# A hybrid trunk block on one core: squares ahead of the projection, and six up-projection units in front instead of four

## The chip, the cores and the metric

The kernel runs on one core of one Trainium2 chip. The core has a matrix engine (PE), a vector engine (DVE), an activation engine (ACT), a general engine (POOL), a queue engine that issues transfers (SP), and DMA engines between HBM and on-chip memory. Each engine works through its own list of instructions in order; semaphores make one wait for another. Matmul results land in eight accumulation banks. The metric is the device time of one execution in microseconds, the median of several runs. Lower is better.

## The reference

One layer of a hybrid block over x of 2048 rows by 1024 columns in float32, then a final RMSNorm:

```python
xn = rmsnorm(x, norm1_g[l])
z = xn @ w_in[l]
u_pool, zq, zf, zi, zo, zg = jnp.split(z, splits, axis=-1)
gates = jax.nn.sigmoid(zg + b_gate[l]).reshape(B, S, N_BRANCHES, D_MODEL)
ya = pool_mixer(u_pool, pool_w[l], pool_scale[l]) @ w_pa[l]
yb = hgrn2_mixer(zq, zf, zi, zo, lower_bounds[l], hgrn_norm_g[l]) @ w_pb[l]
merged = gates[:, :, 0] * ya + gates[:, :, 1] * yb
x = x + merged @ w_o[l]
x = x + conv_glu_ffn(rmsnorm(x, norm2_g[l]), w_up[l], conv_w[l], conv_b[l], w_down[l])
return rmsnorm(x, final_g)
```

The mixers are a causal pooling over windows of 2 to 16 rows and a gated linear recurrence. The feed-forward part (FFN) multiplies by w_up (1024 by 5632), applies a causal convolution of width 3, a SiLU gate, and multiplies by w_down (2816 by 1024).

## The kernel before

**Passes and stages.** The 2048 rows go through in two passes (b0 = 0 and 2) of 1024 rows, each two blocks of 512: the "first rows" and the "second rows". A pass runs proj_io (the columns of w_in for the recurrence's input and output gate), the other projections, the mixers, the output projection (wo), and then ffn: the up-projection in 22 units of 128 value and 128 gate columns, and the down-projection.

**Seven products.** Each product of two-by-two blocks (two halves of the contraction, two blocks of rows or columns) is done with seven block products, P1 to P7, instead of eight, in Strassen's manner. Each needs a form of the rows: P1 B11, P2 B21 (first rows alone), P6 T2, P5 T1, P7 T3, P4 T4, P3 B22 (all with second rows in them). forms_a_task makes B11 and B21, forms_b_task the other five. The weights, too, enter as quarters or sums of quarters.

**Precision.** Each operand is split into a rounded high part and the remainder (`split` for rows, `Stream.convert` for weights: a copy on ACT at line 205, a subtraction on DVE at line 206). A product is three matmuls, high by high, high by low, low by high. A step (one unit, one of P1 to P7) has four parts of three, twelve matmuls of 512 columns.

**Order by ticks.** Every sixth matmul calls tick(), which converts the next weight of the stream, at most LOOKAHEAD = 4 ahead of the step and with N_OPS = 6 buffers, and lets each waiting task emit its next piece. need() makes the task that builds the forms emit what a step needs before the step. What is emitted earlier has priority, and a scheduler then fixes the order of each engine's list. Working tiles are 82 "slots" of one pool (N_SLOTS).

**The opening.** At the end of the program text forms_of("x", 0, ...) makes the two tasks for the first 1024 rows: nxt[1] for the first rows and nxt[2] for the second. nxt[1] is stepped five times (squares, row norms, transposes of the first rows), the loads of the second rows are issued (load_rows(1)), and nxt[1] is run to its end. nxt[2] is not stepped there; the first tick inside proj_io does it. Its first step goes through norm_rows for all four tiles of 128 rows without a pause (lag 0): for each tile two squares with sums on ACT (row_rstd, line 635), a sum and the reciprocal root on POOL (lines 636, 628, 629), two scalings on DVE (line 649). It then waits for go_io, which proj_io sets at the second part of P2, and goes on with transposes on PE and the forms T2, T1, T3, T4 and B22. In proj_io the four results of P1 are copied out of their banks by ACT (io_e, line 1142) before P2 adds to the same banks.

**The FFN's start.** up_order gives the order of the steps. The N_HEADS = 2 first pairs of units, (0, 1) and (2, 3), lead: P1 and P2 of all of them come first, which want the first rows alone; then the other five products, pair by pair. The rest of the units follow interleaved, with a shift of seven steps. GO_AT = 5: from the sixth step on forms_b_task may go on with the second rows. P1's result is copied out (e1, line 1031), P2's too (h, through value, line 991); P6 and P7 leave u2 and u3 (lines 1033, 1037), P4 and P3 close (lines 995, 997). The convolution and the gate of a unit are put on a list, `work`, of which one item is taken per step.

**Names in the views.** x_ and m_ are the rows ahead of the projection and ahead of the FFN; x_f6h is the high part of the seventh tile of the first rows' forms, m_T23l the low part of T2's fourth; io_, fr_, gr_, ur_, up_, wo_ and dn_ are the products, with X, Z and V for the banks; ops are converted weights, raw loaded ones, kw and su weight sums kept in or made in DRAM.

Of the kernel before, what the change touches and what calls it, by code (L numbers as in the profile page):

```python
# [14 lines left out]
AF = mybir.ActivationFunctionType  # L15
# [43 lines left out]

N_SLOTS = 82  # L60
N_RUN = 3
N_HEADS = 2
GO_AT = 5
LEAD = 5
X_AT, X_AT2 = 1, 4
# [7 lines left out]
N_OPS = 6  # L73
# [5 lines left out]
def tile_trunk(  # L79
# [16 lines left out]
    pe, act, dve, pool, sp = nc.tensor, nc.scalar, nc.vector, nc.gpsimd, nc.sync  # L96
# [9 lines left out]
    def slot(name, cols=TB, dt=F32):  # L106
        return slots.tile([P, cols], dt, tag="s", name=name, padded_shape=[P, 528])
# [4 lines left out]
    def f32(ap):  # L112
        return ap.bitcast(F32)
# [26 lines left out]
    def join(task):  # L140
        while task.live:
            task.step()
# [14 lines left out]
    class Stream:  # L157
# [34 lines left out]
        def convert(self):  # L192
            j = len(self.tiles)
            key, fn, raws = self.ops[j]
            while any(r.tile is None for r in raws):
                self.load()
            store_kept()
            v = fn(f"w{j}")
            t = opsp.tile([P, 2, 512], F32R, tag="ops", name=f"ops{j}")
            n = int(np.prod(v.shape[1:]))  # L200
            hi, lo = t[:, 0, :n], t[:, 1, :n]
            if len(v.shape) == 3:
                hi = hi.rearrange("p (a b) -> p a b", a=v.shape[1])
                lo = lo.rearrange("p (a b) -> p a b", a=v.shape[1])
            self.mark = act.copy(hi, v)  # L205
            dve.tensor_tensor(lo, v, f32(hi), ALU.subtract)  # L206
            self.tiles.append((key, t))
            self.load_ahead()
# [21 lines left out]
    def behind(ins, other):  # L230

        tc.add_manual_dep(ins.ins, other.ins.name, mybir.DependencyInfo(
            mybir.DependencyClass.NoSync, mybir.DependencyReason.DATA), reason="behind")

    urgent = [None]

    def first(ins):

        urgent[0] = ins
# [68 lines left out]
    def store_kept():  # L308
        while keeping:
            sp.dma_start(*keeping.pop(0))  # L310
# [110 lines left out]
        return {p: (lambda p=p: plan(p)) for p in ORDER}  # L421

    def up_order():
        heads = [(0, 1), (2, 3), (4, 5)][:N_HEADS]
        res = [(m, p) for ms in heads for p in ("P1", "P2") for m in ms]
        res += [(m, p) for ms in heads for p in ("P6", "P5", "P7", "P4", "P3") for m in ms]

        rest = [(7 * m + 2 * i, m, p) for m in range(2 * N_HEADS, MF)
                for i, p in enumerate(ORDER)]
        return res + [(m, p) for _, m, p in sorted(rest)]  # L430

    def plan_ffn():
        units = {}
        for m, p in up_order():
            if m not in units:
                units[m] = sums_of_unit(w_up_t, m, MF + m,
                                        lambda p, m=m: sums["up"].of(m, SUM_OF[p]))
            fn, raws = units[m][p]()
            stream.op("up", fn, raws)
        plan_rows("dn", w_dn, R_DN, MF // 2)  # L440
# [67 lines left out]
    def load_rows(b):  # L508
        for j in range(NT):
            load_x_tile(b, j)  # L510
# [39 lines left out]
    junk = const.tile([P, 512], F32, tag="junk", name="junk")  # L550
# [6 lines left out]
    def setup_task():  # L557
        pool.memset(uhist, 0.0)
        pool.iota(inv[:, 3], pattern=[[1, 16]], base=1, channel_multiplier=0,
                  allow_small_or_imprecise_dtypes=True)  # L560
        for g, w in enumerate(WINDOWS):
            pool.tensor_scalar(inv[:, g], inv[:, 3], float(w), None, ALU.min)
        flat_inv = inv.rearrange("p a b -> p (a b)")
        dve.reciprocal(flat_inv, flat_inv)
        yield 1
        keys = [(h, h, 0, h) for h in (1, 2, 4, 16)]
        for t, off in ((0, 0), (1, 0)):
            pool.memset(fmask[:, t], 0.0)
            pool.affine_select(out=fmask[:, t], in_=fmask[:, t], compare_op=ALU.not_equal,
                               fill=1.0, base=off, pattern=[[-2, 64]], channel_multiplier=1)  # L570
        keys += [(8 * h + t, 2 * h, t * h, h) for h in (4, 16) for t in range(2)]
        for key, x, off, w in keys:
            nb = 64 // x
            mf = slot(f"mf{key}", 64)
            pool.memset(mf, 1.0)
            v = mf.rearrange("p (b h) -> p b h", h=x)
            pool.affine_select(out=v, in_=v, pattern=[[-2 * x, nb], [0, x]],
                               compare_op=ALU.is_ge, fill=0.0, base=-off, channel_multiplier=1)
            pool.affine_select(out=v, in_=v, pattern=[[2 * x, nb], [0, x]],
                               compare_op=ALU.is_ge, fill=0.0, base=off + w - 1,  # L580
                               channel_multiplier=-1)
            m8 = const.tile([P, 64], U8, tag=f"m{key}", name=f"m{key}")
            yield 2
            dve.tensor_copy(m8, mf)
            masks[key] = m8.rearrange("p (b h) -> p b h", h=x)
        for t in range(2):
            mf = slot(f"mfd{t}", 64)
            pool.memset(mf, 0.0)
            pool.affine_select(out=mf, in_=mf, compare_op=ALU.not_equal, fill=1.0, base=-t,
                               pattern=[[-2, 64]], channel_multiplier=1)  # L590
            m8 = const.tile([P, 64], U8, tag=f"md{t}", name=f"md{t}")
            yield 2
            dve.tensor_copy(m8, mf)
            masks[-1 - t] = m8.unsqueeze(1)
        pool.memset(hist, 0.0)
        for h in range(HEADS):
            pool.memset(state[h, 0], 0.0)
# [28 lines left out]
    def rstd_of(ssq, n, scale, name):  # L626
        r = small.tile([P, 4], F32, tag="rstd", name=name)
        pool.tensor_scalar(r[:, :n], ssq, scale, EPS, ALU.mult, ALU.add)  # L628
        pool.tensor_tensor(r[:, :n], r[:, :n], neghalf[:, :n], ALU.pow)
        return r  # L630

    def row_rstd(halves, junk, name):
        ss = small.tile([P, 4], F32, tag="ssq", name=name + "ss")
        for hf in range(2):
            act.activation(junk[hf], halves[hf], AF.Square, accum_out=ss[:, hf : hf + 1])
        pool.tensor_tensor(ss[:, 2:3], ss[:, 0:1], ss[:, 1:2], ALU.add)
        return rstd_of(ss[:, 2:3], 1, 1.0 / D, name + "r")

    def norm_rows(src, name, xs, after, lag=1):
        for j in range(NT):  # L640
            while (src, j) not in ready:
                yield 1
            halves = [xt[src, j, c] for c in range(2)]
            t = [slot(f"{name}xs{j}_{hf}") for hf in range(2)]
            r = row_rstd(halves, t, f"{name}{j}")
            if lag:
                yield lag
            for hf in range(2):
                dve.tensor_scalar(t[hf], halves[hf], r[:, 0:1], None, ALU.mult)
                xs[j, hf] = t[hf]  # L650
            after(j)
# [101 lines left out]
    def forms_of(kind, b, gain, after=lambda b: lambda j: None, early=False, go=lambda: True):  # L753
        forms = {k: [] for k in ("B11", "B21", "B22", "T1", "T2", "T3", "T4")}
        full = {k: [] for k in ("B11", "B21", "T2")}
        first = Task(forms_a_task((kind, b), gain, forms, full, after(b), early))
        late = Task(forms_b_task((kind, b + 1), gain, forms, full, after(b + 1), go))
        return forms, first, late
# [230 lines left out]
    def value(dst, a, ps):  # L989
        if a is None:  # L990
            act.copy(dst, ps)
            return
        t, how = a
        if how == "from":
            dve.tensor_tensor(dst, ps, t, ALU.subtract)  # L995
        else:
            dve.tensor_tensor(dst, t, ps, ALU.add if how == "add" else ALU.subtract)  # L997
# [382 lines left out]
    def ffn(b0, forms, late):  # L1380
# [15 lines left out]
        def emit_up(m):  # L1396
# [41 lines left out]
            def emit(s, hf, a, ps):  # L1438
                h = slot(f"h{b0}_{m}_{s}_{hf}", 2 + TB)
                hs[s, hf] = h  # L1440
                value(h[:, 2:], a, ps)
                first = (0, 0) if m >= 2 * N_HEADS else (1, 0)
                if (s, hf) == first:
# [103 lines left out]
    nxt = forms_of("x", 0, o_n1, early=True, go=lambda: go_io[0])  # L1547
    for _ in range(5):
        nxt[1].step()
    load_rows(1)  # L1550
    join(nxt[1])
    Task(setup_task())
    lg = cols[:, o_lb : o_lb + 4]
    dve.tensor_tensor(lbt[:, 0], lg, lg, ALU.subtract)
# [5 lines left out]
    for b in range(0, SEQ // TB, 2):  # L1560
# [4 lines left out]
        nxt = ffn(b, forms, late)  # L1565
# [50 lines left out]
```

## Time and profile before

| what | us |
|---|---|
| runs before (3) | 2573.06, 2574.07, 2575.15; median 2574.07 |
| the profiled execution | 2575.64 |
| its span, first to last instruction | 2573.9 |
| PE busy in it | 2519.3 |
| DVE, ACT, POOL busy in it | 1964.0, 1191.9, 851.5 |
| mean granted clock of PE | 0.993 of full |

A row of a timeline or group names start, duration, engine, line of the kernel, operation, and the tiles as out<-in, with shapes and a count; in brackets stands how long the engine was idle before it, and what ended that. PEld is the load of weights into PE. Matmuls overlap: one has a length of 0.39 us in the rows, while the next one starts 0.23 us behind it. Rows of waits and groups are sums over the whole span unless a stretch is given.

### The profile page before, as it was taken

How to read it: one execution, taken by the hardware profiler on the slowest of the kernel's cores; microseconds unless marked ns; L12 is line 12 of the kernel's file. 1: busy time of each engine (PE TensorE's matmuls, PEld its weight loads, DVE VectorE, ACT ScalarE, POOL GpSimd, SP SyncE). 2: the span in 40 equal slices, each digit the busy share in tenths (PEclk: the TensorE clock that was granted, in tenths of full speed). 3: DMA queues.
4: the chain of work that ended last, by engine and by line, in shares of the span. 5: the costliest groups of instructions: out<-in, count | busy, mean ns of one | idle time of the engine just before them, and what ended most of it. 6: DMA issues, size and time to landing. Idle time of an engine off the chain costs nothing.

```text
span 2573.9 us, 35491 instructions
## 1 busy us (share of the span) xinstructions
PE 2519.3 (98%) x11464; PEld 2057.0 (80%) x11464; DVE 1964.0 (76%) x3382; ACT 1191.9 (46%) x2244; POOL 851.5 (33%) x1209
## 2 busy tenths in 40 slices
PE   7899999999999999999999999999999999999998
PEld 6678888788788888878878888888887888888887
DVE  7878788478789777786486776775978987778844
ACT  5335434324555544554364354442355554445533
POOL 6534344031445333462141111200223433334502
PEclk9899999999999999999999999999999999999999
DMA  6787768767788888887364343356442454446942
GB/s 219 254 248 204 210 201 247 215 223 245 179 235 235 235 242 230 252 318 252 107 211 149 99 139 119 120 160 224 143 165 88 151 153 144 144 139 209 366 149 98
DMA packets 254058, 496.88 MB, mean 193 GB/s; under 512 B 26736, under 2 KB 43248, under 8 KB 253552
## 3 DMA queue, kind: packets, MB, share of 16 engines
q1 hardware_dynamic: 187968, 319.89, 38.5%
q0 software_dynamic: 41504, 110.64, 16.8%
q10 hardware_dynamic: 24400, 64.08, 7.3%
q8 instruction: 90, 1.47, 0.2%
q14 instruction: 96, 0.79, 0.1%
HBM read 384.94 MB, written 187.17 MB: 222 GB/s over the span
## 4 chain that ended last, share of the span: by engine, by line
PE 89%; DVE 5%; issue 2%; ACT 2%; DMA 1%; POOL 1%; SPq 0%; DVEq 0%; POOLq 0%; ACTq 0%
PE dn_P L145 16%; PE up_Z L145 14%; PE up_V L145 9%; PE up_X L145 9%; PE wo_P L145 6%; PE gr_Z L145 5%; PE pb L145 3%; PE pa L145 3%; PE gr_X L145 3%; PE gr_V L145 3%; PE fr_Z L145 3%; PE fr_V L145 2%; PE fr_X L145 2%; PE pl L867 1%; PE io_Z L145 1%
## 5 line engine op out<-in xcount | busy, mean ns | idle before, releaser
L205 ACT CAST ops<-raw 128x512 fp32r<-128x512 f32 x732 | 452.7, 620 | 792.9 <-PE dn_P L145 147.6
L206 DVE TENSOR_TENSOR ops<-raw,ops 128x512 fp32r<-128x512 f32 x732 | 555.4, 762 | 207.8 <-ACT ops L205 204.0
L1409 DVE SCALAR_TENSOR_TENSOR e<-h,cols,e 128x512 f32<-128x512 f32 x176 | 142.4, 812 | 30.8 <-ACT e L1407 26.5
L1407 ACT ACTIVATE e<-h,cols 128x512 f32<-128x512 f32 x176 | 142.4, 814 | 29.1 <-DVE h L997 21.0
L1412 DVE SCALAR_TENSOR_TENSOR e<-h,cols,e 128x512 f32<-128x512 f32 x176 | 133.7, 768 | 2.8
L805 POOL DMA_DIRECT2D g_P<-dg_P x154 | 83.3, 543 | 101.3 <-PE dn_P L145 28.5
L1103 POOL TENSOR_TENSOR gf_P<-e,e 128x512 f32<-128x512 f32 x44 | 65.6, 1493 | 153.3 <-DVE e L1418 98.8
L1103 POOL TENSOR_TENSOR gf_P<-gf_P,e 128x512 f32<-128x512 f32 x44 | 59.1, 1344 | 66.6 <-DVE e L1418 66.1
L1402 POOL COPY h<-h 128x2 f32<-128x2 f32 x88 | 39.5, 463 | 121.2 <-DVE h L995 119.2
L1404 POOL COPY hist<-h 128x2 f32<-128x2 f32 x88 | 38.8, 442 | 121.1 <-DVE h L997 119.4
L1416 ACT ACTIVATE e<-e 128x512 f32<-128x512 f32 x88 | 55.6, 632 | 46.2 <-DVE e L1412 46.0
L997 DVE TENSOR_TENSOR h<-up_u,up_V 128x512 f32<-128x512 f32 x88 | 60.0, 682 | 13.3 <-PE up_V L145 12.8
L1212 POOL TENSOR_TENSOR q<-q,qs 128x512 f32<-128x512 f32 x16 | 22.7, 1419 | 139.0 <-ACT qs L1211 127.9
L854 POOL COPY qm<-q 128x64 f32<-128x64 f32 x64 | 24.4, 404 | 117.7 <-DVE q L860 43.9
L1079 DVE TENSOR_TENSOR x<-x,wo_P 128x512 f32<-128x512 f32 x88 | 56.0, 675 | 8.3 <-PE wo_P L145 8.1
L1249 ACT ACTIVATE gt<-gt,cols 128x512 f32<-128x512 f32 x48 | 34.8, 725 | 57.5 <-DVE gt L997 35.1
L1079 DVE TENSOR_TENSOR ac<-ac,dn_P 128x512 f32<-128x512 f32 x72 | 47.3, 682 | 18.4 <-PE dn_P L145 16.5
L1103 POOL TENSOR_TENSOR yf_P<-ya,ya 128x512 f32<-128x512 f32 x16 | 21.1, 1322 | 117.3 <-DVE ya L1326 117.3
L628 POOL TENSOR_SCALAR ro<-so 128x4 f32<-128x4 f32 x16 | 3.2, 199 | 156.8 <-ACT junk L969 156.8
L1477 POOL TENSOR_TENSOR fss<-fss 128x1 f32<-128x1 f32 x16 | 6.6, 415 | 144.2 <-ACT fo L1467 144.2
L1432 POOL DMA_DIRECT2D dg_P<-gf_P x88 | 50.1, 569 | 8.5 <-POOL gf_P L1103 7.7
L1031 ACT COPY up_e<-up_X 128x512 f32<-128x512 f32 x44 | 25.8, 586 | 57.6 <-PE up_X L145 47.5
(1267 smaller groups left out, 8303.4 us busy)
## 6 DMA issues: line engine op xcount, KB each, us to landing
g_P<-dg_P POOLq DMA_DIRECT2D x154, 256.0 KB, 6.4
raw<-in_w_up_t SPq DMA_DIRECT2D x132, 256.0 KB, 3.1
raw<-in_w_in_t SPq DMA_DIRECT2D x98, 256.0 KB, 3.2
dg_P<-gf_P POOLq DMA_DIRECT2D x88, 256.0 KB, 3.8
raw<-in_w_io SPq DMA_DIRECT2D x68, 256.0 KB, 4.8
dg_P<-e SPq DMA_DIRECT2D x66, 256.0 KB, 3.2
raw<-in_w_dn SPq DMA_DIRECT2D x66, 256.0 KB, 4.5
x<-in_x SPq DMA_DIRECT2D x64, 256.0 KB, 5.1
```

The costliest lines, as they stand in the source:

```text
L145: count[1] = pe.matmul(*args, **kw)
L205: self.mark = act.copy(hi, v)
L206: dve.tensor_tensor(lo, v, f32(hi), ALU.subtract)
L805: eng.dma_start(t, d)
L997: dve.tensor_tensor(dst, t, ps, ALU.add if how == "add" else ALU.subtract)
L1079: dve.tensor_tensor(t, t, ps[j], ALU.add if sg > 0 else ALU.subtract)
L1103: pin(pool.tensor_tensor(t, x0, x1, op))
L1407: in_turn(act.activation(t, h[:, 2:], AF.Identity, bias=col(o_cb + mt), scale=col(o_cw + 4 * MF + mt)))
L1409: in_turn(second(dve.scalar_tensor_tensor(t, h[:, 1 : 1 + TB], col(o_cw + 2 * MF + mt), t, ALU.mult, ALU.add)))
L1412: dve.scalar_tensor_tensor(t, h[:, 0:TB], col(o_cw + mt), t, ALU.mult, ALU.add)
L1416: in_turn(act.activation(g, g, AF.Silu))
L1432: pool.dma_start(d, t)
```

## The change

N_HEADS goes from 2 to 3, so that units 0 to 5 lead: twelve steps of P1 and P2 instead of eight come before the first P6, and three pairs run through the other five products instead of two. The first step of nxt[2], with the squares and scalings of the second rows, is emitted in the opening, ahead of everything of the projection. And the first weight conversion from the seventh on (j >= N_OPS) is ordered behind the last of these squares (`opening`): `behind` puts the copy on ACT at line 205 later in ACT's own list, without a semaphore. This happens once in the program. No arithmetic is added or taken away.

```diff
-N_HEADS = 2
+N_HEADS = 3
...
             self.mark = act.copy(hi, v)
+            if j >= N_OPS and opening[0] is not None:
+                behind(self.mark, opening[0])
+                opening[0] = None
             dve.tensor_tensor(lo, v, f32(hi), ALU.subtract)
...
     urgent = [None]
+    opening = [None]
...
-        heads = [(0, 1), (2, 3), (4, 5)][:N_HEADS]
+        heads = [(0, 1), (2, 3), (4, 5), (6, 7)][:N_HEADS]
...
-            act.activation(junk[hf], halves[hf], AF.Square, accum_out=ss[:, hf : hf + 1])
+            ins = act.activation(junk[hf], halves[hf], AF.Square, accum_out=ss[:, hf : hf + 1])
+            if name == "x1_3":
+                opening[0] = ins
...
     load_rows(1)
     join(nxt[1])
+    nxt[2].step()
     Task(setup_task())
```

## The prediction

> **What bounds the kernel now.** I read the page first, then PE's waits, then stretches of time (windows), then the timelines of single engines.
>
> ```profile
> span 2573.9 us, 35491 instructions
> ...
> PE 2519.3 (98%) x11464; PEld 2057.0 (80%) x11464; DVE 1964.0 (76%) x3382; ACT 1191.9 (46%) x2244; POOL 851.5 (33%) x1209
> ...
> PE 89%; DVE 5%; issue 2%; ACT 2%; DMA 1%; POOL 1%; SPq 0%; DVEq 0%; POOLq 0%; ACTq 0%
> ```
>
> PE is busy for 98% and is 89% of the chain that ended last. The change takes no matmul away, so it can win only PE's idle time, 2573.9 - 2519.3 = 54.6 us, and stretches at half clock. The windows (the stretch, its length, PE's busy time with matmuls, granted clock, DMA share, GB/s) show where some of both lies:
>
> ```profile
> 653.52:664.62 11.10, 11.10 (x50) 1.00 1.05 245
> 676.44:694.15 17.71, 13.76 (x50) 0.90 0.85 174
> 694.15:707.77 13.62, 12.14 (x49) 1.00 0.46 153
> 1938.90:1955.29 16.39, 13.62 (x50) 0.90 0.21 65
> 1955.29:1968.95 13.66, 12.17 (x50) 1.00 0.24 78
> 16.85:29.74 12.89, 12.89 (x48) 0.87 0.69 250
> 29.74:52.31 22.57, 16.84 (x81) 0.92 0.39 124
> ```
>
> The edges are starts of steps. The first row is the free pace: four steps of twelve matmuls in 11.10 us, 0.231 each. The next two are the eight steps P6, P5 and P7, P4 of the first pair of FFN units; the two after them the same in the second pass. P6 and P5 lose 17.71 - 11.10 = 6.61 and 16.39 - 11.10 = 5.29; P7 and P4 lose 2.52 and 2.56. The last two rows are the opening: P1 of the first projection without a gap, then P2, which takes 22.57.
>
> **Six units lead.** PE's timeline names the first of these losses:
>
> ```profile
> 679.97 0.51 PE L145 MATMUL up_Z<-m_T23h,ops 128*128 128x512 f32 x1 [1.29 <-ACT m_T23h L606]
> 681.61 0.51 PE L145 MATMUL up_Z<-m_T23l,ops 128*128 128x512 f32 x1 [1.14 <-DVE m_T23l L607]
> 683.69 0.63 PE L145 MATMUL up_Z<-m_T21l,ops 128*128 128x512 f32 x1
> 688.29 0.50 PE L145 MATMUL up_V<-m_T11l,ops 128*128 128x512 f32 x1 [0.68 <-DVE m_T11l L607]
> 690.09 0.50 PE L145 MATMUL up_V<-m_T12l,ops 128*128 128x512 f32 x1 [0.84 <-DVE m_T12l L607]
> ```
>
> P6 wants form T2 of the second rows, whose four parts ACT, DVE and POOL make one behind the other:
>
> ```profile
> 666.39 0.69 ACT L723 ACTIVATE m_b<-m_t,negs 128x512 f32<-128x512 f32 x1 [0.46 <-PE m_t L655]
> 679.95 1.61 DVE L607 TENSOR_TENSOR m_T23l<-m_t,m_T23h 128x512 fp32r<-128x512 f32 x1
> 680.82 0.59 ACT L991 COPY h<-up_X 128x512 f32<-128x512 f32 x1
> 682.43 0.62 ACT L205 CAST ops<-raw 128x512 fp32r<-128x512 f32 x1 [1.02 <-issue]
> ```
>
> The chain ends at 679.95 + 1.61 = 681.56; PE reaches P6 at 676.44. The change puts four more steps, P1 and P2 of units 4 and 5, in front of that P6 and leaves GO_AT at 5, so the chain starts where it did and P6 comes 48 x 0.231 = 11.1 later, at 687.5: slack 6.0. T1 is wanted by P5 at 693.1 instead of 682 plus the stalls. T10 and T11 are emitted before that; T13 is still made at the last moment, at P5's first step, but is wanted there only at the tenth matmul, 2.1 later, against 0.6 + 0.7 of work. So I take the whole 6.61 and 5.29 away, 11.9.
>
> What it adds: no instruction, only an order. Units 4 and 5 hold four more tiles, e1 and h, and their P2 adds to the bank that e1's copy must first read. That copy comes behind the h copy that ends at 680.82 + 0.59 = 681.4, lasts as long, and P2 of unit 4 starts at 682.0: between 0, and 0.6 if the cast of the row after it goes first. I take 0.3 per pass. P7 and P4 keep their 2.5, since T3 and T4 are emitted at the same distance before use; bounds 0 (hidden too) and twice that. The sum streams (DRAM adds on ACT's and POOL's queues) are asked for later or at the same step: unit 4's first sum at step 32 instead of 29, unit 5's at 33 instead of 34. **Term: -11.9 + 0.6 = -11.3 us**, bounds -16.4 and -6.
>
> The slow clock is in it. Right behind the T23 stalls the matmuls are 0.63 long at a pace of 0.43, and the windows give 0.90; 0.10 of 17.71 and of 16.39 is 3.4 us in all. The Trainium skill, TensorE: Matmul & The Clock Gate, section "Why this matters for your kernels", asks for no PE-idle gaps over about 3 us, and these gaps are 1.3 and 1.1, so by its rule they would not cost the clock. The trace has the slow stretch behind this stall in both passes, so I go by the trace; the other reading is a rival below.
>
> **The squares and the tied conversion.** ACT, then POOL, in the opening:
>
> ```profile
> 24.93 0.62 ACT L205 CAST ops<-raw 128x512 fp32r<-128x512 f32 x1 [6.69 <-PE io_X L145]
> 25.45 0.68 ACT L663 ACTIVATE x_b<-x_t,cols 128x512 f32<-128x512 f32 x1
> 26.55 0.69 ACT L663 ACTIVATE x_b<-x_t,cols 128x512 f32<-128x512 f32 x1
> 31.42 0.62 ACT L635 ACTIVATE x_xs<-x 128x512 f32<-128x512 f32 x1
> 32.03 2.01 ACT L1142 COPY io_e<-io_X 128x512 f32<-128x512 f32 x4
> 26.22 0.62 POOL L604 TENSOR_SCALAR x_f6h<-x_b 128x512 fp32r<-128x512 f32 x1 [4.77 <-ACT x_b L663]
> 27.32 1.14 POOL L604 TENSOR_SCALAR x_f7h<-x_b 128x512 fp32r<-128x512 f32 x1 [0.48 <-ACT x_b L663]
> 40.20 0.54 POOL L629 TENSOR_TENSOR x_3r<-x_3r,neghalf 128x1 f32<-128x1 f32 x1
> 19.38 1.05 POOL L604 TENSOR_SCALAR x_f4h<-x_b 128x512 fp32r<-128x512 f32 x1
> ```
>
> The cast at 24.93 is the seventh (six are in flight, N_OPS). It holds ACT for 6.69 us until PE frees a pair, and two x_b copies, the eight squares and the four io_e copies queue behind it. Tied behind the last square, it lets them past: x_b at 18.2 and 18.8, squares from 19.4 to 19.4 + 8 x 0.61 = 24.4. Their rows have come by then:
>
> ```profile
> L504 SPq DMA_DIRECT2D x<-in_x x16: 327/328/432, 0.8 to 15.6; - x16
> DMA to landing us min/median/max: 3.4/5.3/6.0
> ```
>
> The last is issued at 15.6 and lands by 21.6, while the squares are in their fourth. The cast then still starts at 24.93, so its wait costs nothing; behind it on ACT are the eighth cast and io_e, on DVE its remainder, on SP the load that reuses its raw buffer, all on time. If the squares were late, the cover is long: P2 wants this pair at about 31, and cast and remainder take 1.4. The step moved ahead issues squares, sums, rstd and scalings; no DMA, and it passes none on SP or POOL.
>
> What PE gets:
>
> ```profile
> 32.74 0.71 PE L145 MATMUL io_X<-ops,x_f4h 128*128 128x512 f32 x2 [3.00 <-ACT io_e L1142]
> 42.96 1.41 PE L655 MATMUL x_t<-ident,x_xs 128*128 128x128 f32 x9 [0.94 <-DVE x_xs L649]
> 52.31 0.72 PE L145 MATMUL io_Z<-ops,x_T20h 128*128 128x512 f32 x2 [1.78 <-DVE x_t L712]
> 48.62 1.91 PE L655 MATMUL x_t<-ident,x_xs 128*128 128x128 f32 x16
> 90.08 1.19 PE L145 MATMUL io_Z<-ops,x_T40h 128*128 128x512 f32 x2 [4.31 <-DVE io_u L1148]
> ```
>
> io_e no longer waits for the squares, so P2 starts at 29.74, 3.0 earlier, and the half clock behind that gap (0.08 of 22.57, 1.8 us) goes. But P6 at 52.31 hangs on the second rows: rstd on POOL, scaling on DVE, transposes, T2. POOL works without a break from x_f7h (ends 28.46) through masks and weight sums to the last rstd at 40.74, so that row of work moves by what POOL waited for: 4.77 + 0.48 = 5.25, less 0.4 because x_f6h then runs beside DVE, as x_f4h does (1.05 instead of 0.62). **Term: -4.8 us.** The lower end is 0, if what follows eats it (rival 1). The upper end is 7.7, PE alone: P2 from 29.74 with 48 x 0.231 and two times 1.91 of transposes ends at 44.6, and 52.31 - 44.6 = 7.7. What is late next is DVE's u3, for which PE waits at 90.08. DVE is busy nearly all of the time from 44.5 to there, so I let its end move along with its start:
>
> ```profile
> 44.53:90.00 45.47, 44.06 (x58) 0.98 0.66 226
> ```
>
> **Sum**: -11.3 - 4.8 = -16.1. The profiled execution took 2575.64 (span 2573.9 and 1.7 around it) and would take 2559.5. The median of the runs is 1.6 lower, 2574.07, which gives **2558.0 us**.
>
> **Rivals.**
>
> 1. The opening gives its gain back: the 4.31 at 90.08 grows to 9.1, because weight sums and loads, not the second rows, set DVE's pace. For it: DVE is the engine waited for there. Against: those sums stand in the same queue and move too. Only the lead remains: 2574.07 - 11.3 = 2562.8.
> 2. The stall in the FFN moves on: T1 and T3 are emitted just before use and P7 is reached without the pause in which DVE caught up. Then only the T23 stalls with their clock go (2.4 + 1.7 per pass, 8.2 together) and P7 pays some 1.5 each, as much as T11 and T12 did: 2574.07 - 4.8 - 8.2 + 3 = 2564. Against: the 6.0 of slack.
> 3. The clock rule of above holds, and the slow stretches come anyway: 3.4 less, 2561.4.
> 4. Slower: the 82 slots run out. They are given out in program order, so one that isn't free holds all later ones. The seven forms take 56, six leading units 12 instead of 8, the pair at work about 10: 78 by my count, 74 before. From 83 on each evacuation of P4 and P3 waits for a convolution to free a slot, which is one ACTIVATE and two DVE operations of
>
> ```profile
> L1409 DVE SCALAR_TENSOR_TENSOR e<-h,cols,e 128x512 f32<-128x512 f32 x176 | 142.4, 812 | 30.8 <-ACT e L1407 26.5
> L1407 ACT ACTIVATE e<-h,cols 128x512 f32<-128x512 f32 x176 | 142.4, 814 | 29.1 <-DVE h L997 21.0
> ```
>
> some 2.4 us; eight per pass and two passes are 38: 2574.07 - 16.1 + 38 = 2596. For it: the work left over peaks at 12 items instead of 10. Against: four slots spare.
> 5. The order comes out otherwise and nothing is won: about 2574.
> 6. More: P7 and P4 lose their 2.5 as well, and the opening gives 7.7: 2574.07 - 11.9 - 5.1 - 7.7 = 2549.4.
>
> **How the numbers follow.** Forecast 0.57, rival 1 0.13, 2 0.09, 3 0.03, 4 0.07, 5 0.06, 6 0.05. The range runs from 2551, between forecast and rival 6, to 2566, past rivals 1 to 3; left out are rivals 4 to 6, 0.18. About 0.2%, 5 us, is what a measurement of this kernel can tell from no change. Faster by more: 0.57 + 0.13 + 0.09 + 0.03 + 0.05 = 0.87; within: 0.06; slower: 0.07.
>
> **What would show it.** Right: PE's waits without m_T23h and m_T23l; twelve up_X steps without a gap before the first up_Z; no half clock behind them; on ACT the eight squares ahead of the seventh cast and no 6.69 before it; P2 close to 29.7, P6 near 47.5. Wrong: PE idle at P7's start (rival 2), over 8 us before P4 of the projection (rival 1), evacuations on DVE that wait for e tiles (rival 4).

## The result and the profile after

| | before | after |
|---|---|---|
| runs | 2573.06, 2574.07, 2574.30, 2575.15 | 2558.99, 2559.36, 2560.58, 2565.47 |
| median | 2574.19 | 2559.97 |
| profiled execution, its span | 2575.64, 2573.9 | 2560.58, 2558.7 |
| PE busy | 2519.3 | 2514.9 |

The ratio is 0.9949, with a 95% interval of 0.9932 to 0.9967: 14.2 us less (8.5 to 17.5). Forecast were 16.1 less and 2558.0. Five more runs of the changed kernel beside the experiments gave a median of 2561.66 against 2572.57, ratio 0.9959 (0.9946 to 0.9971), 10.9 less (7.5 to 13.9). The forecast lies inside the first interval and outside the second. An estimate from the two is a gain near 13, which makes the forecast some three microseconds too good.

The FFN's start came out as the working has it. In the windows of the changed kernel (stretch, length, PE busy, ..., granted clock) the eight steps of the first pair now are:

```profile
681.63:692.76 11.13, 11.13 (x49) 8.93 (x48) 8.03 (x11) 6.09 (x11) 2.72 (x2) 1.00 0.94 271
692.76:706.42 13.66, 12.19 (x49) 8.70 (x48) 13.29 (x21) 7.46 (x13) 4.14 (x8) 1.00 0.46 154
1939.32:1950.40 11.08, 11.08 (x49) 8.94 (x48) 8.03 (x11) 6.10 (x11) 2.73 (x2) 1.00 0.32 108
1950.40:1964.03 13.63, 12.15 (x49) 8.70 (x48) 13.29 (x21) 7.37 (x13) 3.89 (x7) 1.00 0.24 79
```

P6 and P5 run at the free pace in both passes (11.13 and 11.08 instead of 17.71 and 16.39), at full clock. P7 and P4 kept their loss (13.66 and 13.63; before 13.62 and 13.66). PE's waits in the first pass, 640 to 730 us, show one new wait, for up_e (e1); the other three stood there before:

```profile
PE up_Z L145 <- DVE up_u L1043: 1.0, 2, 0.6
PE up_X L145 <- ACT up_e L1037: 0.3, 1, 0.3
PE up_Z L145 <- DVE m_T43l L611: 0.2, 1, 0.2
PE up_Z L145 <- DVE m_T42l L611: 0.2, 1, 0.2
```

No row names m_T23h, m_T23l, m_T11l or m_T12l any more. (The lines of the changed kernel stand 3 to 6 further down than before.) In the opening ACT does what was forecast:

```profile
18.97 0.68 ACT L639 ACTIVATE x_xs<-x 128x512 f32<-128x512 f32 x1
...
23.78 0.23 ACT L639 ACTIVATION_READ_ACCUMULATOR x_xs<-x 128x1 f32 x1
26.03 1.31 ACT L205 CAST ops<-raw 128x512 fp32r<-128x512 f32 x2 [2.02 <-PE io_X L145]
28.79 2.67 ACT L1148 COPY io_e<-io_X 128x512 f32<-128x512 f32 x4 [1.45 <-PE io_X L145]
```

The eight squares run from 18.97 to 24.0 (forecast 19.4 to 24.4), the cast waits behind them, and io_e waits for PE, no longer for the squares. P2 starts at 30.67 instead of 32.74, and not at 29.7 as forecast: P1 lay under two slow windows of the clock (16.0 to 22.8) where the kernel before had one (16.8 to 20.2). And of the second rows' gain less arrives at PE than on POOL. POOL's last rstd, then PE's timeline with the starts of P2 and P6 and the wait for u3:

```profile
35.74 0.59 POOL L633 TENSOR_TENSOR x_3r<-x_3r,neghalf 128x1 f32<-128x1 f32 x1
```

```profile
30.67 0.63 PE L145 MATMUL io_X<-ops,x_f4h 128*128 128x512 f32 x2
...
49.78 0.95 PE L145 MATMUL io_Z<-ops,x_T20h 128*128 128x512 f32 x2 [1.46 <-DVE x_t L718]
...
87.72 0.77 PE L145 MATMUL io_Z<-ops,x_T40h 128*128 128x512 f32 x1 [2.20 <-DVE io_u L1154]
```

The last rstd ends at 36.33 instead of 40.74, 4.4 earlier; P6 starts at 49.78 instead of 52.31, only 2.5 earlier.

**A gain that nobody forecast.** Both programs issue the same number of PE instructions, so the start of the n-th one can be compared. Up to 456 us the changed kernel is 3.1 ahead; at 470 it is 7.3 ahead. There the kernel before waited, in PE's and ACT's timelines:

```profile
463.56 0.50 PE L145 MATMUL gr_Z<-x_T30h,ops 128*128 128x512 f32 x1 [2.37 <-DVE gr_u L1033]
461.56 0.62 ACT L606 CAST mxs_2h<-mx 128x512 fp32r<-128x512 f32 x1 [7.95 <-DMA mx<-md]
```

A load of mx kept a cast on ACT waiting; its remainder stands ahead of gr_u on DVE, and PE waits for gr_u. The change touches none of these instructions.

### The profile page after: what moved, and what is told of

It is laid out like the page before. It is cut to its first block, busy times and chain, and to the rows that moved or that the text cites. A ratio compares the mean times of both kernels' runs of the same rounds, so it can differ in the third digit from the quotient of the medians.

```text
span 2558.7 us, 35497 instructions
## 1 busy us (share of the span) xinstructions
PE 2514.9 (98%) x11464; PEld 2053.2 (80%) x11464; DVE 1976.1 (77%) x3382; ACT 1189.7 (46%) x2244; POOL 861.4 (34%) x1209
## 3 DMA queue, kind: packets, MB, share of 16 engines
q0 software_dynamic: 41504, 110.64, 16.9%
## 4 chain that ended last, share of the span: by engine, by line
PE 90%; DVE 4%; DMA 2%; POOL 2%; issue 1%; ACT 1%; SPq 0%; DVEq 0%; POOLq 0%; ACTq 0%
PE dn_P L145 15%; PE up_Z L145 14%; PE up_V L145 10%; PE up_X L145 9%; PE wo_P L145 6%; PE gr_Z L145 5%; PE pb L145 3%; PE pa L145 3%; PE gr_X L145 3%; PE gr_V L145 3%; PE fr_Z L145 2%; PE io_Z L145 2%; PE pl L873 2%; PE fr_X L145 1%; PE fr_V L145 1%
## 5 line engine op out<-in xcount | busy, mean ns | idle before, releaser
L209 DVE TENSOR_TENSOR ops<-raw,ops 128x512 fp32r<-128x512 f32 x732 | 547.6, 751 | 192.4 <-ACT ops L205 187.5
L1415 DVE SCALAR_TENSOR_TENSOR e<-h,cols,e 128x512 f32<-128x512 f32 x176 | 150.7, 859 | 22.7 <-ACT e L1413 20.4
L1418 DVE SCALAR_TENSOR_TENSOR e<-h,cols,e 128x512 f32<-128x512 f32 x176 | 139.2, 798 | 2.7
```

The lines of the kernel that those rows point to most:

```text
L1415: in_turn(second(dve.scalar_tensor_tensor(t, h[:, 1 : 1 + TB], col(o_cw + 2 * MF + mt), t, ALU.mult, ALU.add)))
L1418: dve.scalar_tensor_tensor(t, h[:, 0:TB], col(o_cw + mt), t, ALU.mult, ALU.add)
```

## The experiments

All edits are against the changed kernel, except e8. The table adds up each profile against the first profile of before: how much earlier the same PE instruction starts, in us. "To 135" is the 450th instruction (134.7 us in that profile). The next columns are what is won from 456 to 470 (instructions 2060 to 2110), and across the two starts of the FFN (first up_X of the pass to instruction 3400, 651 to 765 us; first up_X of the second pass to instruction 9124, 1913 to 2025). The last column is the whole of it at PE's last matmul (2566), with the other stretches in it.

| kernel | to 135 | 456 to 470 | FFN 1 | FFN 2 | at the end |
|---|---|---|---|---|---|
| after | 3.3 | 4.2 | 5.9 | 4.8 | 15.3 |
| after again (e9) | 1.5 | 3.0 | 5.9 | 4.8 | 11.3 |
| before again (e8) | -2.5 | 4.2 | 0.0 | 0.0 | 2.4 |
| e1 lead alone | 0.0 | 2.8 | 5.9 | 4.6 | 13.8 |
| e2 squares alone | 3.5 | 2.3 | -0.3 | 0.9 | 3.4 |
| e3 no tie | -2.4 | -0.5 | 5.8 | 4.7 | 5.0 |
| e4 eight lead | 2.1 | -0.5 | 3.2 | 2.5 | 7.1 |
| e5 later chain | 5.9 | 2.6 | 2.4 | 0.3 | 9.3 |
| e6 T1 sooner | 1.9 | 0.3 | 7.7 | 6.8 | 13.2 |
| e11 T1 sooner, again | 1.5 | 4.2 | 7.8 | 6.8 | 16.9 |
| e7 masks later | 7.2 | -1.6 | 5.9 | 4.8 | 14.7 |
| e10 both | 4.6 | 4.2 | 7.9 | 6.8 | 21.8 |
| e12 sums on POOL | 3.5 | 2.9 | 6.0 | 4.7 | 11.7 |

Among kernels with the same FFN edit the two FFN columns repeat to 0.3. They jump only where the slow clock comes or stays away (e2's second pass, e5's first). The first two columns vary by 4 to 5 among kernels that run the same order of instructions up to there, since their edits all lie further on (after, e4, e5, e6, e9, e11). The last column is less than the four before it together: 2.9 less in the changed kernel, 3.0 in e2, 3.8 in e9, while e1 and e8 lose nothing. This goes in small pieces over the span, and its cause stays open.

### e1: the lead alone

```diff
-                opening[0] = ins
+                pass
...
-    nxt[2].step()
```

> The changed kernel without the early step and without the tie: six units lead, the opening is that of the kernel before. Theory: the two parts are independent, and the lead alone takes what the traces show at the two starts of the FFN, 6.0 and 4.8, so 2574.2 - 10.8 = 2563.4, with the first up_Z free of waits for m_T23h and m_T23l, a wait for up_e of 0.3 per pass, and the opening at the times of before (P6 near 52.3, u3 wait 4.3). Rival: the opening is worth nothing in the end, and the lead alone gives the whole 14 (2560). Second rival: the 2.37 of idle time and the half clock at 461 to 467, which the profile of before has and that of the changed kernel hasn't, belong to the kernel with the old opening: then this profile shows them again, otherwise they were one execution's transfers.

Measured: 2562.70 (2561.89 to 2567.48) against 2573.75, ratio 0.9957 (0.9944 to 0.9969), 11.05 less. The FFN columns are those of the changed kernel, the opening is that of before (P6 at 52.68, u3's wait 4.90). The time alone does not exclude the first rival, since the changed kernel's second measurement gained 10.9, no more than this. The trace speaks against it: the opening column is 0.0 here, and 1.5 or more wherever the squares are tied. The second rival falls: the stall at 461 is short here with the old opening (table: 2.8 of the 4.2 won).

### e2: the squares alone

```diff
-N_HEADS = 3
+N_HEADS = 2
```

> The changed kernel with four leading units: only the early step and the tie are left. Theory: the opening is worth the 3.2 that the traces show up to 146 us, so 2574.2 - 3.2 = 2571.0, and the stalls for m_T23h and m_T23l stand as before. Rival: the opening also takes away the stall at 461 (4.2), which then is missing here and gives 2566.8. Second rival: worth nothing, 2574.2.

Measured: 2571.36 (2570.52 to 2574.60, 11 runs) against 2573.75, ratio 0.9992 (0.9983 to 1.0000), 2.4 less, half of the forecast 4.8; the interval just touches no change. With e1's 11.05 that makes 13.4, which lies between the two measurements of the whole (10.9 and 14.2), so nothing here speaks against adding the parts.

### e3: the early step without the tie

```diff
-                opening[0] = ins
+                pass
```

> The changed kernel with the early step but without the tie: the seventh and eighth casts stand ahead of the last two x_b copies on ACT again. Theory: the tie is what frees ACT, the early step alone brings nothing, since the squares then still queue behind the 6.7 of waiting: a 6 to 7 us wait before the seventh cast, io_e's first copy at 31 or later, P6 near 52, time as with the lead alone, 2563.4. Rival: the early step alone does it, 2560.

Measured: 2565.98 (2563.66 to 2570.79), ratio 0.9962 (0.9949 to 0.9976): 3.3 above e1, so the early step alone brings nothing; whether it costs is not shown, since the two ranges of times overlap. ACT's timeline of e3:

```profile
26.25 0.62 ACT L205 CAST ops<-raw 128x512 fp32r<-128x512 f32 x1 [8.39 <-PE io_X L145]
26.78 0.68 ACT L669 ACTIVATE x_b<-x_t,cols 128x512 f32<-128x512 f32 x1
...
33.36 2.01 ACT L1148 COPY io_e<-io_X 128x512 f32<-128x512 f32 x4
```

The cast holds ACT for 8.39 again, x_b and the squares queue behind it, io_e starts at 33.36 (before 32.03) and P6 at 55.62. Emitting work earlier does not pull it past an instruction that waits in the same list; the tie does.

### e4: eight units lead

```diff
-N_HEADS = 3
+N_HEADS = 4
```

> The changed kernel with eight leading units instead of six. Live slots at the start of the FFN by program order are 80 of 82 (76 with six, 72 with four). Theory: the first pair's P6 and P5 are already free of stalls, so only P7's and P4's loss (1.5 of idle time per pass, 2.5 with the pace) can still go, and each further pair that leads adds one wait for e1 of 0.3: between 2555.5 and 2560.6. Rival (slots): the eight evict something and P4 or P3 wait for free tiles, 2565 or more.

Measured: 2565.46 (2563.09 to 2568.88), ratio 0.9963 (0.9951 to 0.9976): by the FFN columns 5 worse than six. It is not the slots: in the two stretches of the FFN's starts no evacuation waits more than 0.2 for anything but PE. The waits for m_T42l and m_T43l are gone and one for u3 has grown. DVE's timeline of e4, then PE's:

```profile
714.32 0.69 DVE L209 TENSOR_TENSOR ops<-raw,ops 128x512 fp32r<-128x512 f32 x1 [0.88 <-ACT ops L205]
714.93 0.69 DVE L611 TENSOR_TENSOR m_T43l<-m_t,m_T43h 128x512 fp32r<-128x512 f32 x1
715.53 0.68 DVE L611 TENSOR_TENSOR m_B223l<-m_b,m_B223h 128x512 fp32r<-128x512 f32 x1
716.13 0.68 DVE L1043 TENSOR_TENSOR up_u<-up_Z,up_e 128x512 f32<-128x512 f32 x1
```

```profile
716.96 0.48 PE L145 MATMUL up_Z<-m_T40h,ops 128*128 128x512 f32 x1 [3.33 <-DVE up_u L1043]
```

The first u3, which must empty PE's bank, stands behind a conversion that waits and behind the last two remainders of the forms; PE loses 3.33, and 1.7 more at half clock (718.1 to 721.5).

### e5: the chain starts as late against P6 as before

```diff
-GO_AT = 5
+GO_AT = 9
```

> The changed kernel with GO_AT at 9 instead of 5: six units lead, but the second rows' chain of forms starts four steps (11.1 us) later, as far ahead of P6 as it stood in the kernel before. Theory (distance is all): the chain ended at 675.1 with P6 at 681.6, so it now ends 4.6 late, about what it was late before (5.1), and the losses of before come back with the waits for m_T23h and m_T23l and a slow stretch behind them: 2560 + 10 = 2570, FFN starts gaining 0 to 1.5 per pass against the kernel before instead of 6.0 and 4.8. Rival (more of the independent work in front fills the gap by itself): no stall, 2560.

Measured: 2569.92 (2566.20 to 2576.04, 11 runs) against 2574.70, ratio 0.9988 (0.9978 to 0.9998). The waits of before are back to a tenth, in the first pass:

```profile
PE up_Z L145 <- ACT m_T23h L610: 1.3, 1, 1.3
PE up_Z L145 <- DVE m_T23l L611: 1.1, 1, 1.1
PE up_Z L145 <- DVE up_u L1043: 1.1, 2, 0.6
PE up_V L145 <- DVE m_T12l L611: 0.7, 1, 0.7
```

So the distance between the chain and P6 is the whole of the lead's effect. The 2.4 that the first pass still wins against before is 1.7 of half clock that did not come (see the clock below) and the wait for m_T11l of 0.68, which is missing here.

### e6 and e11: T1 emitted faster

```diff
             forms["T1"].append(split(t1[k], f"{name}T1{k}"))
-            yield 5
+            yield 2 if src[0] == "m" else 5
```

> The changed kernel, with the pause behind each part of T1 cut from 5 ticks to 2 in the FFN: T1, T3, T4 and B22 are emitted in the time that the six units' lead leaves, and by program order all their remainders stand on DVE ahead of the first u3 instead of two pairs between the first u3 and the second. Theory: the 1.5 of idle time at P4 of the first pair (two waits for up_u, two for m_T42l and m_T43l), 2.5 with the pace, goes in both passes: 2560 - 5 = 2555, and the eight units lost because that queue stood ahead of u3. Rival: the remainders come to stand ahead of u2 instead and P7 waits for u2, or P6 and P5 get the losses back: 2560 or more.

> T1's pause of 2 ticks alone, again, beside the changed kernel on the same chip. Theory: 4 us below the changed kernel of this call, and the first pair of units in the FFN without a wait before P4 again. Rival: the new wait of 0.8 for e1 (0.3 in the changed kernel) and what follows eat it: 2 or less.

Measured: 2558.94 (2556.21 to 2564.50), ratio 0.9945 (0.9931 to 0.9958), and 2558.73 (2555.26 to 2562.54), ratio 0.9943 (0.9929 to 0.9956), the latter 2.9 below the changed kernel measured beside it (2561.66). The intervals of the ratios overlap, so the times alone do not show the gain; the traces do. In the changed kernel four remainders stand ahead of the second u3 on DVE:

```profile
700.38 0.68 DVE L611 TENSOR_TENSOR m_T42l<-m_t,m_T42h 128x512 fp32r<-128x512 f32 x1
700.99 0.68 DVE L611 TENSOR_TENSOR m_B222l<-m_b,m_B222h 128x512 fp32r<-128x512 f32 x1
701.59 0.68 DVE L611 TENSOR_TENSOR m_T43l<-m_t,m_T43h 128x512 fp32r<-128x512 f32 x1
702.19 0.68 DVE L611 TENSOR_TENSOR m_B223l<-m_b,m_B223h 128x512 fp32r<-128x512 f32 x1
702.79 0.68 DVE L1043 TENSOR_TENSOR up_u<-up_Z,up_e 128x512 f32<-128x512 f32 x1
```

With the faster T1 they are done before the first u3, and PE's waits of the first pass in e6 are one row:

```profile
PE up_X L145 <- ACT up_e L1037: 0.8, 1, 0.8
```

The traces gain 1.8 to 2.0 per pass over the changed kernel, less than the 2.5 expected: the wait for e1 grew by 0.5.

### e7: the masks out of the second rows' way

```diff
         dve.reciprocal(flat_inv, flat_inv)
-        yield 1
+        yield 14
```

> The changed kernel with the masks of the setup task put off by 13 ticks (some 18 us), so that POOL's list from x_f7h to the last rstd holds the weight sums alone. Theory (POOL's list sets when the second rows' chain starts): the last rstd comes 4 to 5 us earlier than 36.3, and P6 starts that much before 49.8, with 1 to 4 of it left at 134 us: 2556 to 2559. Rival (the rest of the opening's gain is given back at DVE, which has the weight sums, forms and u3 to do up to 88): P6 moves and the wait for u3 grows by as much, time unchanged, 2560. Second rival: rstd doesn't move, since other work holds it.

Measured: 2559.68 (2557.85 to 2562.79) against 2574.70, ratio 0.9946 (0.9933 to 0.9958). POOL's and PE's timelines of e7:

```profile
31.54 0.67 POOL L633 TENSOR_TENSOR x_3r<-x_3r,neghalf 128x1 f32<-128x1 f32 x1
46.37 1.21 PE L145 MATMUL io_Z<-ops,x_T20h 128*128 128x512 f32 x2 [1.46 <-DVE x_t L718]
```

The last rstd ends 4.1 earlier than in the changed kernel, P6 starts 3.4 earlier, and at 135 us the profile is at 7.2, against 1.5 to 5.9 in the eight with the squares tied and the masks in their place. So POOL's list does set when the second rows start, and the masks are part of it. From rstd to P6 it takes 14.16 here instead of 13.45, so a part is given back again. The time does not tell this kernel from the changed one (15.0 less here; 14.2 and 10.9 there).

### e8 and e9: both kernels again

> The kernel before, unchanged, for a second profile of it. Theory: the 2.37 of idle time before gr_Z<-m... at 463.6 (a load of mx that took 8.6 us to land) is a matter of the single execution, since two of the four kernels tried so far have it with either opening; here it can be there or not, and its length differs. Rival: it belongs to the old opening and comes back with the same length. The stalls at the two starts of the FFN are to be the same to a tenth, and the opening's wait for io_e again 3.0.

> The changed kernel, unchanged, beside the next two. Theory: 0.994 to 0.996 of the kernel before (2558 to 2564), with the same waits at the two starts of the FFN and an opening that gains 1 to 5 at 134 us against the first profile of before, since the four profiles with this opening so far gave 1.9 to 5.9.

Measured: 2576.14 (2569.79 to 2577.28, 11 runs) for the kernel before, ratio 1.0000 (0.9989 to 1.0011); 2561.66 (2559.97 to 2566.44) for the changed one, ratio 0.9959 (0.9946 to 0.9971). In e8 PE goes through the place of the stall without a gap:

```profile
462.04 0.40 PE L145 MATMUL gr_X<-x_f7h,ops 128*128 128x512 f32 x1
462.27 0.40 PE L145 MATMUL gr_Z<-x_T30h,ops 128*128 128x512 f32 x1
```

Here the cast waits 5.31 for the load of mx instead of 7.95. The same program has the stall in one execution and not in the next; the 4.2 belong to the transfers of that execution.

### e10: both edits together

```diff
-        yield 1
+        yield 14
...
-            yield 5
+            yield 2 if src[0] == "m" else 5
```

> The changed kernel with both later edits: T1's pause of 2 ticks in the FFN, and the masks put off by 13 ticks. Theory (the gains add): T1's pause gave 2.0 per pass at the two starts of the FFN in its trace, the masks some 2 to 4 in the opening, so 5 to 8 us below the changed kernel of the same call, about 2553 to 2556. Rival (the opening gives it back by 134 us): 4 below it. Second rival (the time of such edits is lost in what varies from execution to execution): no difference that the intervals tell.

Measured: 2555.49 (2551.78 to 2558.24) against 2572.57, ratio 0.9930 (0.9918 to 0.9942); 6.2 below the changed kernel measured beside it, with intervals that do not overlap, and the fastest kernel here. The FFN's 2.0 per pass are there again; of the opening's part one profile, 4.6 at 135 us, cannot say how large it is.

### e12: two weight sums from DVE to POOL

```diff
-                        (dve if i == (p == "P6") and p != "P5" and p != "P7" else pool
+                        (dve if i == (p == "P6") and (p, k) not in (("P6", 2), ("P6", 3)) and p != "P5" and p != "P7" else pool
```

> The changed kernel with the second addition of two weight sums, w10s and w11s (P6's third and fourth parts of the contraction, first pass), on POOL instead of DVE. Theory (work of DVE that does not move with the second rows now stands in their way: between the last rstd and P6 DVE's w10s and the remainders behind it take 2.46 and 1.40 of 13.45, before 0.83 and 0.14 of 11.57): P6 comes 1.5 to 2.5 earlier than in the two profiles of the changed kernel (49.78 and 50.21), some 11.5 behind the last rstd, and the time falls by 0 to 2. Rival (DVE's operations get longer beside POOL's two-input additions, or the order hardly matters): 13 or more between the last rstd and P6.

Measured: 2561.91 (2559.49 to 2564.00) against 2576.27, ratio 0.9943 (0.9929 to 0.9957), like the changed kernel. From the last rstd (36.02) to P6 (50.37) it takes 14.35, not less: my theory falls. Two rows of DVE's timeline of e12, of work that is there in both kernels:

```profile
38.78 1.27 DVE L588 CAST m<-mf 128x64 uint8<-128x64 f32 x1
47.04 1.76 DVE L611 TENSOR_TENSOR x_T21l<-x_t,x_T21h 128x512 fp32r<-128x512 f32 x1
```

The same cast is 0.27 and the same remainder 0.68 in the changed kernel. Both are long while POOL adds (w10s from 38.55 to 40.00, w14s from 46.88 to 48.24), and both end only when that addition is through, the remainder 0.56 after it. The additions taken off DVE cost it time all the same.

## Why the prediction was right, and where not

**The FFN's start: right.** Forecast -11.3 (-6.3 and -5.0 by pass); the traces show 5.9 and 4.8, the runs of e1 11.05. Each step held. The end of the chain (a row of one tile: shortest, median and longest in ns, then the first and last start) and the wait for e1 in the changed kernel:

```profile
L611 DVE TENSOR_TENSOR m_T23l<-m_t,m_T23h x1: 1617/1617/1617, 673.5 to 673.5; 128x512 fp32r<-128x512 f32 x1
```

```profile
675.99 0.50 PE L145 MATMUL up_X<-m_f4h,ops 128*128 128x512 f32 x1 [0.26 <-ACT up_e L1037]
```

The chain ends at 673.5 + 1.6 = 675.1 and P6 starts at 681.63, slack 6.5 (forecast 6.0). e1's wait is 0.26 (forecast 0.3). T1 and T3, made at the last moment, cost nothing. P7 and P4 keep 2.5. e5 takes the distance away and the old waits return.

**The opening: right mechanism, size too large.** Forecast -4.8; e2's runs give -2.4 (0 to -4.4), and the traces at 135 us 1.5 to 5.9 for seven profiles with the squares tied and the masks where they were (after, e2, e4, e5, e6, e9, e11; mean 2.8) against -2.5 to 0.0 for three with the old opening (before, e1, e8; mean -0.8), which is 3.6. The term that was mis-sized is "so that row of work moves", taken as far as P6. POOL's part did: the last rstd comes 4.4 earlier. But from there to P6 (its start less the end of rstd, as in 49.78 - 36.33) the three old openings take 11.56 to 11.65 and those seven 13.41 to 13.45: some 1.85 is given back there in every execution. PE waits for the same x_t in both kernels. DVE's timeline of the kernel before, from ahead of rstd to that x_t and just behind:

```profile
38.35 0.68 DVE L206 TENSOR_TENSOR ops<-w9s,ops 128x512 fp32r<-128x512 f32 x1
...
50.05 0.69 DVE L338 TENSOR_TENSOR w10s<-w10s,raw 128x512 f32<-128x512 f32 x1
...
51.50 0.75 DVE L712 SCALAR_TENSOR_TENSOR x_t<-x_t,cols,x_t 128x512 f32<-128x512 f32 x1
52.17 0.68 DVE L206 TENSOR_TENSOR ops<-w10s,ops 128x512 fp32r<-128x512 f32 x1
```

and of the changed kernel, from the end of rstd on:

```profile
36.60 0.72 DVE L209 TENSOR_TENSOR ops<-w9s,ops 128x512 fp32r<-128x512 f32 x1
...
43.06 1.78 DVE L342 TENSOR_TENSOR w10s<-w10s,raw 128x512 f32<-128x512 f32 x1
...
46.27 0.68 DVE L209 TENSOR_TENSOR ops<-w10s,ops 128x512 fp32r<-128x512 f32 x1
...
48.98 0.75 DVE L718 SCALAR_TENSOR_TENSOR x_t<-x_t,cols,x_t 128x512 f32<-128x512 f32 x1
```

The sum w10s is 1.1 longer, its conversion stands ahead of that x_t instead of behind it, and that of w9s falls into the stretch. The weight work on DVE moved too, but by other amounts than the 4.4 of rstd: the conversion of w9s by 1.75, the sum w10s by 7.0 and its conversion by 5.9. So all three now stand between rstd and that x_t, where before it was the sum alone. Why the order came out so no run shows. That the sum alone is the cause did not stand up (e12, where other operations grew in its place); how much is the order on DVE and how much the longer operations beside POOL's additions stays open.

**Rival 1**, that the wait for u3 grows from 4.31 to 9.1, was wrong in its place: it shrank to 2.20. But something was given back, and on DVE among the weight sums as this rival had it, only earlier, ahead of P6. What the prediction held against it, that those sums move too, is true but no help, since they did not move by the same amount as the rows. **Rival 2** fell with e1: P7 is no later. **Rival 3** is answered below. **Rival 4** fell: with six units no evacuation waited for anything but PE at the FFN's starts, and what e4 lost with eight was DVE's order. (The prediction counts 78 live slots with six units and e4's expectation 76; no run tests either count.) **Rivals 5 and 6** fell by the time; the loss of P7 and P4 that rival 6 wanted gone needed one more edit (e6).

**What the sum lacked.** The first profile of before holds 4.2 of stall at 461 to 467 that the second profile of the same program lacks (e8). A difference of two profiles would have ascribed it to the change; the forecast, made from single steps, did not contain it.

## What to carry to other kernels

A stall that comes from a chain being late goes away when independent work is put in front by more than the lateness; how much is read from the end of the chain and the start of its first use, and moving the chain's start back is the test. To bring work forward on an in-order engine, look for the instruction that waits in front of it: here the early step without the tie was worth nothing. Where a row of work is moved, ask on every engine that it passes what does not move with it, or moves by another amount, and compare profiles only after a second profile of the same kernel has shown what varies by itself.

## What the hardware showed

**The slow clock goes by fixed windows.** In all 14 profiles, the very end left out, the slow stretches (granted clock 0.50) start whole multiples of 3.413 us from one another and last one or two of them. The kernel before and e5 have the same stall, 1.3 for m_T23h and 1.1 for m_T23l. Cut at the edges of these windows, the kernel before (PE busy is the second number, the clock the third from the end) shows

```profile
679.00:682.41 3.41, 1.30 (x4) 0.86 (x5) 3.10 (x5) 2.11 (x4) 3.00 (x4) 1.00 1.10 257
682.41:685.82 3.41, 3.41 (x9) 2.63 (x8) 3.40 (x2) 1.14 (x2) 3.41 (x4) 0.50 0.64 89
```

and e5, in its first pass,

```profile
679.10:682.50 3.40, 2.13 (x9) 1.22 (x7) 3.21 (x5) 1.40 (x4) 1.19 (x2) 1.00 0.67 164
682.50:685.90 3.40, 2.27 (x11) 1.81 (x11) 3.17 (x4) 2.16 (x5) 3.40 (x5) 1.00 0.38 120
685.90:689.30 3.40, 3.07 (x13) 2.00 (x11) 3.40 (x5) 2.01 (x4) 1.35 (x1) 1.00 0.81 281
```

Where the stall falls into one window, PE is idle for 2.11 of it and the next one runs at half clock, which costs 1.7; where an edge parts it, 1.27 and 1.13, nothing follows. Counted over the 14 profiles from 14 us to 2540 us, 53 windows at full clock were followed by a slow one, and PE was idle for 1.68 to 3.41 us in each; of those with more than 1.90 idle none went without, and from 1.68 to 1.90 it went either way. So about half a window of idle time, in several short gaps, is enough. The Trainium skill, TensorE: Matmul & The Clock Gate, section "What's actually happening", has a free-running window of 3413 ns, and the traces agree; its rule in "Why this matters for your kernels", no idle gaps over some 3 us, is not enough here: the kernel before had gaps of 1.29 and 1.14, with 0.97 and 1.14 of them in one window, and the next window was slow. So rival 3 goes by phase: the 3.4 in the forecast are worth 1.7 or nothing per pass, by chance. In the four profiles that have the old stall (before, e8, e2, e5) the slow window came in six of eight passes.

**Executions of one program differ by 10 us.** 69 runs of the kernel before lie between 2569.66 and 2580.12, median 2574.47. Its two profiles differ at the stall at 461, where the load of mx lands later in one, and in the opening, where e8 has eight slow windows up to 135 us and the first profile six. At 1.7 each that would be 3.4; the table has 2.5. Why the slow windows differ there is not shown.
